# Gathering key and value pages behind the rotary tables' loads, with the page table in a small tile of its own

## The chip, the cores and the metric

The kernel runs on one core of a Trainium2 chip. The metric is the time of one execution on the device in microseconds (us). Engines are named as in the profile: PE is TensorE's matmul stream, PEld its weight loads, DVE is VectorE, ACT is ScalarE, POOL is GpSimd, SP is SyncE. TensorE's clock has two levels, 2.4 GHz (shown as 1.00) and 1.2 GHz (0.50).

## What is computed

One inference step of a two-layer decoder trunk on a prompt of 1024 tokens and 8 sample tokens, f32 in and out. Layer 0 mixes tokens with retention and with a sparse attention whose keys an indexer selects; layer 1 is a gated DeltaNet. Each layer has a modulated mixer and a squared-ReLU MLP. The part that matters here is the indexer of layer 0, and that the sample tokens have a paged cache of 512 past rows (4 pages of 128 rows for each of 8 samples), each row holding key, value and indexer key:

```python
rel = jax.nn.relu(jnp.einsum('bqhd,bkd->bqhk', qi, ki_all).astype(jnp.float32))
score = jnp.einsum('bqhk,bqh->bqk', rel, wi.astype(jnp.float32)) * IDX_DIM ** -0.5
score = jnp.where(causal[None], score, NEG_INF)
_, idx = lax.top_k(score, top_k)
...
k_sel, v_sel = k_all[bidx, idx], v_all[bidx, idx]
logits = jnp.einsum('bqhd,bqkd->bqhk', q, k_sel).astype(jnp.float32) * ATT_DIM ** -0.5
```

## The kernel before

All activations stand transposed, features on partitions and 1032 tokens along the free axis. A dense product is three matmuls per weight block (high part by high part, high by low, low by high, line 188), so that f32 accuracy comes out of a faster matmul type; weights come by SP's DMAs (line 175), and ScalarE and VectorE split them (lines 176, 177).

The token mixer of layer 0 starts in `even_proj`. It projects the index queries and index key (`iqT`, `ikT`), applies the rotary tables (`rope`, its last VectorE step is line 945), reloads two table tiles `cs` from the DRAM input `tabs` (line 1049) and a block of constants (line 155), and transposes the indexer weights into `iwn`. Then a loop (lines 1059 to 1076) makes the prompt's index scores: for each of six row blocks, up to two stretches of 512 keys and four heads there is one matmul with 64 rows (line 1067) into one of two PSUM banks, a Relu that evicts it on ScalarE (line 1070), and a multiply-add on VectorE. These are called score products below.

`gather_pages` (lines 1445 to 1454) copies the sample's pages out of the pool. It loads the page table into SBUF (line 1449), and then, 32 times, GpSimd reads one entry into a register (line 1453) and starts a copy of one page, 160 KB, from DRAM to DRAM into the buffers `pages0` to `pages7` (line 1454). The page table lies in `kn_`, tile W3, which is also scratch for the rope of the second index query. `sample_scores` then takes, for each sample, the index keys of its four pages (`load_pages`, line 1458, in turn into W2 and W3), transposes them (line 1496), multiplies (line 1499), and ends with the scores `SS` (line 1504). In W3 lie also the index keys that line 1082 writes out, so page 1's load comes after that output. `SS` and the prompt's scores feed a search for the threshold (32 rounds, from line 1366 on; line 1385 compares once a round), which runs on VectorE and ScalarE beside the dense products of the attention projections AV and AQ that follow.

The order of each engine's instructions is that of a scheduler at build time, which takes the program's order, priorities and its own estimates. So an instruction that moves in the program moves others. GpSimd issues in its order: DMAs on tables, gathers, page loads and outputs stand in one queue, and one that waits holds those behind it.

```python
self.gather_pages(kn_[0:1, 768:800])
...
v = nc.gpsimd.value_load(ptab[0:1, 4 * b + i:4 * b + i + 1], min_val=0, max_val=a['cache_kv'].shape[1] - 1)
nc.gpsimd.dma_start(self.pages[b][i], a['cache_kv'][0][bass.ds(v, 1)].rearrange("o p r -> (o p) r"))
```

Of the kernel before, what the change touches and what calls it, by code (L numbers as in the profile page):

```python
# [133 lines left out]
class _Step:  # L134
# [852 lines left out]
    def even_proj(self, mis, w, S, SS, aqS, akS, avS, aqD, akD, vD):  # L987

        nc, tc, a = self.nc, self.tc, self.a
# [6 lines left out]
        cs = t(N[8], N[9])  # L996
        rq, rk = _ring(*t(W[4], W[5])), _ring(*t(N[10], W[0]))
        rg_, vn_, kn_ = t(W[1], W[2], W[3])
# [47 lines left out]
        self.blk = BLK  # L1046
        self.consts(1, N[5])
        for i in range(2):
            nc.gpsimd.dma_start(cs[i], a['tabs'][i])
        iwn = mis(128, 9, 4)  # L1050
        p = self.side('tn')
        for c in range(9):
# [6 lines left out]
        for r in range(2, 8):  # L1059
            n = 128 * (r + 1)  # L1060
            for k0 in range(0, n, 512):
                kw = min(512, n - k0)
                dst = S[r][:, k0:k0 + kw]
                for h in range(4):
# [4 lines left out]
                    x = on().rearrange("p c e -> p (c e)")  # L1069
# [6 lines left out]
            nc.vector.tensor_tensor(dst, dst, self.c('cm'), op=OP.min)  # L1076


        self.gather_pages(kn_[0:1, 768:800])
        self.natural(ikT, kn_[:, :512].rearrange("p (c r) -> p c r", c=8), 'tn', rows=64)  # L1080
        kv = a['kv_prompt'][0, 0].rearrange("(c p) r -> p c r", p=128)
        nc.gpsimd.dma_start(kv[:, :, 256:320], kn_[:, :512].rearrange("p (c r) -> p c r", c=8))
# [1148 lines left out]
```

## Time and profile before

| what | value |
| --- | --- |
| median of 3 runs | 2978.12 us (2976.19 to 2978.9) |
| the profiled execution | 2991.83 us |
| its span, first to last instruction | 2990.2 us |
| mean granted clock of TensorE | 0.981 |
| busy: PE / DVE / ACT / POOL | 96% / 66% / 42% / 8% of the span |

The profile is of one execution, 13.7 us above the median of the runs. Times inside it count from its first instruction. A row of the stage table gives, for a stretch, each engine's busy time and the granted clock; a row of the timeline gives one instruction or several equal ones in a line (x4), with the idle time ahead of it in brackets and what ended that; a row of waits says which instruction waited for whom. Line numbers are those of the kernel before.

### The profile page before, as it was taken

What the parts mean: (1) busy time and instruction counts of PE and PEld (TensorE: products, weight loads), DVE (VectorE), ACT (ScalarE), POOL (GpSimd) and SP (SyncE); (2) the same over time, 40 slices, a digit from 0 to 9 for tenths busy, and PEclk for the clock granted to TensorE, in tenths of its full rate; (3) what the DMA queues carried; (4) which work ended last, traced back from release to release, by engine and by line L of the source; (5) the groups of instructions that cost most, each with busy time, mean ns of one, the idle gap of its engine ahead of it and who ended that gap; (6) DMA issues with size and microseconds to landing.
All of it is one profiled execution on the core that took longest, in us unless ns stands there. A gap on an engine that the chain in (4) does not pass through costs nothing. (4 is left out here: it accounts for less than half of the span.)

```text
span 2990.2 us, 57153 instructions
## 1 busy us (share of the span) xinstructions
PE 2878.2 (96%) x22980; PEld 2684.1 (90%) x22980; DVE 1966.3 (66%) x5147; ACT 1245.8 (42%) x2498; POOL 240.8 (8%) x328
## 2 busy tenths in 40 slices
PE   8999999999899999999999999999999999999997
PEld 6559997799799999999988999999998999999997
DVE  4569897448755765454677766764768657765557
ACT  4457734426733431111364565542348434321111
POOL 0210002100000000000001111111100000000002
PEclk9989998999999999999999999998999999999998
DMA  8665325213433556552221222223524426343222
GB/s 277 189 201 142 86 72 177 78 50 106 155 121 128 194 168 191 170 164 94 62 83 40 65 62 49 60 77 113 170 82 129 158 96 205 124 141 106 72 71 65
DMA packets 282678, 358.50 MB, mean 120 GB/s; under 512 B 49494, under 2 KB 230523, under 8 KB 281644
## 3 DMA queue, kind: packets, MB, share of 16 engines
q1 hardware_dynamic: 258786, 272.86, 30.3%
q0 software_dynamic: 23296, 81.85, 8.4%
q8 instruction: 180, 2.95, 0.4%
q14 instruction: 86, 0.70, 0.1%
q10 hardware_dynamic: 330, 0.13, 0.0%
HBM read 271.45 MB, written 80.12 MB: 118 GB/s over the span
## 5 line engine op out<-in xcount | busy, mean ns | idle before, releaser
L188 PE MATMUL bank<-XH,whi 128*128 128x256 f32 (+4 forms) x3488 | 906.3, 305 | 1.9 <-ACT N L1268 0.8
L188 PE MATMUL bank<-XH,wlo 128*128 128x384 f32 (+5 forms) x2720 | 825.5, 304 | 0.9 <-DVE wlo L177 0.9
L188 PE MATMUL bank<-XL,whi 128*128 128x256 f32 (+5 forms) x2976 | 792.6, 302 | 2.2 <-DVE XL L426 1.9
L188 PEld LDWEIGHTS bank<-XH,whi 128*128 128x128 f32 (+1 forms) x3488 | 604.2, 188 | 24.2 <-issue 11.1
L188 PEld LDWEIGHTS bank<-XL,whi 128*128 128x128 f32 (+1 forms) x2976 | 525.7, 188 | 17.8 <-issue 9.5
L188 PEld LDWEIGHTS bank<-XH,wlo 128*128 128x128 f32 (+2 forms) x2720 | 511.7, 188 | 7.8 <-issue 5.0
L638 DVE SCALAR_TENSOR_TENSOR N<-bank,G,N 128x256 f32<-128x256 f32 x576 | 274.8, 481 | 312.6 <-PE bank L188 311.5
L176 ACT CAST whi<-raw 128x1024 fp32r<-128x1024 f32 x142 | 147.5, 1039 | 443.2 <-PE bank L188 397.8
L188 PE MATMUL bank<-W,whi 128*128 128x260 f32 (+1 forms) x1152 | 207.7, 282 | 2.9 <-DVE accS L646 1.5
L177 DVE TENSOR_TENSOR wlo<-raw,whi 128x1024 fp32r<-128x1024 f32 x142 | 173.2, 1220 | 45.6 <-ACT whi L176 44.8
L704 PE MATMUL bank<-W,whi 128*128 128x256 f32 x1094 | 182.9, 284 | 12.4 <-ACT whi L697 7.3
L704 PE MATMUL bank<-W,wlo 128*128 128x256 f32 x1082 | 182.0, 284 | 9.5 <-ACT wlo L697 4.2
L704 PE MATMUL bank<-XH,whi 128*128 128x260 f32 x896 | 181.2, 285 | 8.1 <-ACT N L719 3.0
L704 PE MATMUL bank<-XH,wlo 128*128 128x260 f32 x896 | 181.2, 285 | 4.4 <-DVE wlo L691 3.0
L188 PEld LDWEIGHTS bank<-W,whi 128*128 128x128 f32 x1152 | 176.0, 188 | 8.3 <-DVE N L638 2.5
L697 ACT CAST whi<-raw 128x512 fp32r<-128x512 f32 x168 | 103.9, 622 | 170.9 <-PE bank L704 60.3
L704 PEld LDWEIGHTS bank<-W,whi 128*128 128x128 f32 x1094 | 155.0, 188 | 18.8 <-ACT whi L697 9.5
L704 PEld LDWEIGHTS bank<-W,wlo 128*128 128x128 f32 x1082 | 154.5, 188 | 14.6 <-ACT wlo L697 5.7
L188 PE MATMUL bank<-W,wlo 128*128 128x256 f32 (+1 forms) x576 | 162.0, 283 | 0.5 <-DVE wlo L177 0.5
L691 DVE TENSOR_TENSOR whi<-raw,whi 128x512 fp32r<-128x512 f32 x168 | 115.1, 688 | 67.4 <-ACT whi L697 63.6
L697 ACT CAST wlo<-raw 128x512 fp32r<-128x512 f32 x168 | 103.3, 621 | 133.8 <-PE bank L704 50.4
L691 DVE TENSOR_TENSOR wlo<-raw,wlo 128x512 fp32r<-128x512 f32 x168 | 114.6, 687 | 63.0 <-ACT wlo L697 60.5
(628 smaller groups left out, 5461.0 us busy)
## 6 DMA issues: line engine op xcount, KB each, us to landing
raw<-in_mlp_up_dram SPq DMA_DIRECT2D x96, 512.0 KB, 4.2
N<-in_ada_w_dram SPq DMA_DIRECT2D x80, 512.0 KB, 5.3
W<-hD SPq DMA_DIRECT2D x64, 516.0 KB, 4.4
raw<-in_mlp_down_dram SPq DMA_DIRECT2D x60, 512.0 KB, 3.5
hD<-N POOLq DMA_DIRECT2D x32, 520.0 KB, 4.0
N<-resD SPq DMA_DIRECT2D x32, 512.0 KB, 4.6
hD<-N POOLq DMA_DIRECT2D x32, 512.0 KB, 3.6
raw<-in_odd_w_in_dram SPq DMA_DIRECT2D x32, 512.0 KB, 4.2
```

The lines of the kernel that those rows point to most:

```text
L176: nc.scalar.copy(hi[:, :k * m], raw[:, :k * m])
L177: nc.vector.tensor_tensor(lo[:, :k * m], raw[:, :k * m], hi[:, :k * m], op=OP.subtract)
L188: self.nc.tensor.matmul(out, ww[:, i, ms], xx[:, c0:c1], start=start and i == 0 and j == 0, stop=stop and i == nk - 1 and j == 2)
L638: nc.vector.scalar_tensor_tensor(r, ps[:, :256], g[:, dt, 0:1], r, op0=OP.mult, op1=OP.add)
L691: sub = lambda o, x, y: V.tensor_tensor(o, x, y, op=OP.subtract)
L697: nc.scalar.copy(hi, a)
L704: nc.tensor.matmul(o, ww[:, k], xx, start=start and k == 0 and n == 0, stop=k == 3 and n == 2, skip_group_check=True)
```

## The change

`gather_pages` is called right behind the two loads of the rotary tables, and no longer after the score loop. `issue_after(x.ins)` lets the scheduler issue its instructions only behind the second table's load. The page table goes into a piece of 32 words of the tile of small things (`mis`, M), where it was part of W3. Nothing else is edited; lines of the changed kernel are 2 higher from line 1050 to the end of the score loop, and 1 higher from there on.

```diff
         for i in range(2):
-            nc.gpsimd.dma_start(cs[i], a['tabs'][i])
+            x = nc.gpsimd.dma_start(cs[i], a['tabs'][i])
+        with tc.issue_after(x.ins):
+            self.gather_pages(mis(1, 32))
         iwn = mis(128, 9, 4)
...
-        self.gather_pages(kn_[0:1, 768:800])
         self.natural(ikT, kn_[:, :512].rearrange("p (c r) -> p c r", c=8), 'tn', rows=64)
```

On GpSimd, from the tables' loads on, the order before is this (TENSOR_LOAD reads a page table entry, `N_97` is the block of constants, `W_90` is W3):

```order
L1049 DMA N_99<-in_tabs_dram 128x1032
L155 DMA N_97<-in_cst_dram 128x951
L1482 DMA iwD<-M 8x4
L1483 DMA W_96<-iwD 32x1
L1449 DMA W_90<-in_page_table_dram 1x16x2
L1453 TENSOR_LOAD W_90
L1453 ISA x2
L1454 ISA
L1454 DMA pages_994<-in_cache_kv_dram 16x2560
```

And after the change:

```order
L1049 DMA N_99<-in_tabs_dram 128x1032
L1450 DMA M<-in_page_table_dram 1x16x2
L1454 TENSOR_LOAD M
L1454 ISA x2
L1455 ISA
L1455 DMA pages_857<-in_cache_kv_dram 16x2560
L1454 TENSOR_LOAD M
L1454 ISA x2
L1455 ISA
L1455 DMA pages_857<-in_cache_kv_dram 16x2560
L155 DMA N_97<-in_cst_dram 128x951
```

The page table and two of the 32 gathers now stand ahead of the constants' load, 30 behind it; the index weights' detour through DRAM (iwD) has gone behind the gathers. At the end of the gathers the order is, after the change:

```order
L1455 DMA pages_864<-in_cache_kv_dram 16x2560
L1083 DMA out_dram<-W_90 128x8x64
L1483 DMA iwD<-M 8x4
L1459 DMA W_89<-pages_857 128x4x64
L1459 DMA W_90<-pages_858 128x4x64
L1484 DMA W_96<-iwD 32x1
L1459 DMA W_89<-pages_859 128x4x64
```

Before, the page loads followed the output of W3 in the same way, without the two iwD rows between them.

On PE the orders are the same up to row 531. There the order before goes on as follows (rows 529 to 536), with products of AV (128x264):

```order
L188 MATMUL bank_69<-XH,wlo_83 128x384
L1067 MATMUL bank_73<-N_100,W_92 128x512
L1067 MATMUL bank_74<-N_100,W_92 128x512
L188 MATMUL bank_70<-XH,whi_80 128x264
L188 MATMUL bank_70<-XL,whi_80 128x264
L188 MATMUL bank_70<-XH,wlo_83 128x264
L188 MATMUL bank_70<-XH,whi_80 128x264
L188 MATMUL bank_70<-XL,whi_80 128x264
```

After the change the pages' transposes stand there (rows 529 to 539):

```order
L188 MATMUL bank_69<-XH,wlo_83 128x384
L1069 MATMUL bank_73<-N_100,W_92 128x512
L1069 MATMUL bank_74<-N_100,W_92 128x512
L1497 MATMUL bank_71<-cst,W_89 64x128 x4
L1497 MATMUL bank_72<-cst,W_90 64x128
L1069 MATMUL bank_73<-N_100,W_91 128x128
L1497 MATMUL bank_72<-cst,W_90 64x128 x2
L1069 MATMUL bank_74<-N_100,W_91 128x128
L1497 MATMUL bank_72<-cst,W_90 64x128
L188 MATMUL bank_70<-XH,whi_80 128x264
L1500 MATMUL bank_76<-W_89 32x512
```

The first page's transposes have moved from row 583 to row 532, with 28 score products still to come. Between rows 532 and 594 stand all eight pages' transposes and products and 8 matmuls of line 188; before, rows 532 to 637 held 54 of line 188 among them, 24 of 128x264 and 30 of 128x384. The rest of AV follows in one piece from row 596 (128x264), and the search's rounds begin earlier among VectorE's and ScalarE's instructions. From the attention on, the orders agree.

## Rows read from the trace of the kernel before

**Rows 1.** Page of the profile, part 1: busy us and share by engine.

```profile
PE 2878.2 (96%) x22980; PEld 2684.1 (90%) x22980; DVE 1966.3 (66%) x5147; ACT 1245.8 (42%) x2498; POOL 240.8 (8%) x328
```

**Rows 2.** Stages: length, busy us (instructions) by engine, clock, DMA share, GB/s.

```profile
117.20:139.70 22.50, 22.19 (x77) 10.54 (x76) 15.73 (x31) 14.82 (x32) 9.58 (x19) 1.00 0.52 156
139.70:146.50 6.80, 0.00 (x0) 0.00 (x0) 2.28 (x3) 0.98 (x2) 2.93 (x4) 0.62 0.69 183
146.50:165.20 18.70, 18.66 (x45) 7.50 (x46) 6.51 (x13) 3.88 (x7) 3.68 (x6) 0.50 0.26 84
...
400.00:475.00 75.00, 71.24 (x489) 69.50 (x488) 73.48 (x202) 16.83 (x34) 5.87 (x9) 1.00 0.31 87
```

**Rows 3.** Timeline of GpSimd (POOL), 60 to 152 us: start, length, line; idle before.

```profile
72.34 0.53 POOL L1049 DMA_DIRECT2D N<-in_tabs_dram  x1 [8.82 <-PE bank L416]
81.40 0.54 POOL L155 DMA_DIRECT2D N<-in_cst_dram  x1 [8.54 <-DMA resD<-N]
...
95.86 0.51 POOL L1449 DMA_DIRECT2D W<-in_page_table_dram  x1 [3.85 <-DVE W L945]
103.00 0.50 POOL L1454 DMA_DIRECT2D pages<-in_cache_kv_dram  x1 [6.63 <-DVE N L1072]
...
111.53 0.49 POOL L1454 DMA_DIRECT2D pages<-in_cache_kv_dram  x1 [1.06 <-issue]
...
139.78 0.49 POOL L1454 DMA_DIRECT2D pages<-in_cache_kv_dram  x1 [0.67 <-issue]
140.47 0.94 POOL L1082 DMA_DIRECT2D out_dram<-W  x1 [0.21 <-issue]
141.40 0.91 POOL L1458 DMA_DIRECT2D W<-pages  x1
145.89 0.75 POOL L1458 DMA_DIRECT2D W<-pages  x1 [3.58 <-DMA out_dram<-W]
```

**Rows 4.** What PE waited for, 60 to 190 us: total, times, longest.

```profile
PE bank L1496 <- DMA W<-pages: 6.9, 1, 6.9
```

**Rows 5.** Timeline of PE, 105 to 180 us: start, length, line; idle before.

```profile
117.19 0.39 PE L188 MATMUL bank<-XH,whi 128*128 128x264 f32 x1
117.42 0.28 PE L188 MATMUL bank<-XL,whi 128*128 128x264 f32 x1
...
146.54 0.85 PE L1496 MATMUL bank<-cst,W 128*64 128x128 f32 x3 [6.89 <-DMA W<-pages]
...
152.11 1.91 PE L1499 MATMUL bank<-W 64*32 64x512 f32 x2
...
172.05 1.04 PE L1499 MATMUL bank<-W 64*32 64x512 f32 x2
173.11 0.63 PE L1496 MATMUL bank<-cst,W 128*64 128x128 f32 x4
```

**Rows 6.** What weight loads waited for, 117.2 to 139.7 us.

```profile
PEld bank L1067 <- ACT N L1070: 6.8, 14, 0.8
```

**Rows 7.** GpSimd DMAs, 103 to 140 us: KB each, median us to landing.

```profile
pages<-in_cache_kv_dram POOLq DMA_DIRECT2D x32, 160.0 KB, 2.5
```

**Rows 8.** GpSimd DMAs, 146 to 156 us, same columns.

```profile
W<-pages POOLq DMA_DIRECT2D x3, 128.0 KB, 2.6
```

**Rows 9.** PE by stretches: length, busy us, granted clock, DMA share, GB/s.

```profile
38.80:42.30 3.50, 3.50 (x16) 0.51 1.05 317
```

**Rows 10.** VectorE (DVE) by stretches, same columns.

```profile
80.00:100.00 20.00, 13.16 (x18) 1.00 0.68 185
103.00:140.00 37.00, 25.56 (x47) 1.00 0.64 190
```

**Rows 11.** What PE waited for, 177.5 to 475 us.

```profile
PE bank L1234 <- ACT N L1226: 5.0, 4, 2.4
PE bank L1285 <- DVE N L1280: 1.7, 1, 1.7
```

**Rows 12.** Timeline of DVE, 174 to 186 us.

```profile
179.06 0.17 DVE L1385 TENSOR_TENSOR M<-M 128x7 f32<-128x7 f32 x1
```

## The prediction

> **What bounds the kernel now.** The profiled execution took 2991.83 us (span 2990.2). TensorE is busy 2878.2 us, 96% [rows 1], so time is won or lost only where it waits, where its matmuls run longer than they need, or where its clock is low. I went from the stage table to the waits, then to the two timelines that meet at the stop.
>
> The stage table [rows 2] shows one hole: from 139.7 to 146.5 us PE executes nothing. The table of PE's waits gives it one cause, 6.9 us for the first page tile [rows 4]. The GpSimd timeline says why it is late [rows 3]: the 32 gathers run from 103.00 to 139.78, one every 36.78 / 31 = 1.186 us, though each lands in about 2.5 us [rows 7]; the issuing is the limit. The loop begins only after the page table, issued at 95.86 behind DVE's rope (L945, whose output shares the buffer), and PE has score products enough to run until 139.7. The chain ends 141.40 (page 0's load) to 146.54 (transpose): 5.14 us.
>
> Behind the hole lies a second loss. The granted clock is 0.50 (1.2 GHz) from 146.5 to 165.2, 18.70 us, of which PE is busy 18.66 [rows 2]. A page's key product takes 1.91 us there and 1.04 us at full clock [rows 5]. So 18.70 us at half clock did 9.35 us of work. The whole late gather costs 6.9 + 9.35 = 16.25 us.
>
> The third loss is small: from 117.2 to 139.7 the score products alternate over two PSUM banks and each waits for its Relu eviction on ScalarE, 14 waits and 6.8 us in the weight loads' table [rows 6]. PE is shown busy 22.19 of 22.5 us there [rows 2], so a product that waits there must count as a long one.
>
> **The change, part by part.** *The gather moves up on GpSimd.* No instruction is added but one tile M; the page table no longer waits for L945. The last rotary table is issued at 72.34 to 72.87 [rows 3], so the page table's DMA issues there. From page table issue to first gather took 103.00 - 95.86 = 7.14 us; hence first gather at 80.0, at 82.5 if its landing is late. After two gathers the constants' DMA (L155) waits for what it waited for before, and was ready at 81.40, so costs only its issue of 0.54. Thirty gathers at 1.186 us end at about 117.8. Then the index-key output (0.94, it was already waiting in line before), the iwD issue (about 0.5), and page 0's load is issued at about 119.5. With the 5.14 us seen, PE could resume at 124.7; with the late ends 127.5.
>
> *The page work moves up on PE too*, because the scheduler re-planned with an earlier gather: the first transposes stand at row 532 instead of 583. PE passes row 531 at 117.19 [rows 5]. So the gather comes 22 us earlier and its consumer 22 us earlier as well: the wait is 124.7 - 117.2 = 7.5. Page 1's buffer is the one the index keys are written out from, so its load waited 145.89 - 140.47 = 5.42 us from that output's issue [rows 3]; now that ends at 118.0 + 5.4 = 123.4, and with the 2.6 us of a page load [rows 8] page 1 is there at 126.0, when the 0.63 us of page 0's transposes [rows 5] are over for 0.7, of which I count 0.5 as a wait. In all 8.0 against 6.9, **+1.1**. If the page table lands late, +3.9; if output and pages land sooner, at best about -1, since one load's 2.6 us after 119.5 is the least.
>
> *The score stretch is filled.* After the wait the 28 remaining score products share PE's order with 8 page rounds, each a key product of 1.04 and transposes of 0.63, that is 8 x 1.67 = 13.4 us of work [rows 5] between products that waited 6.8 us for evictions. The AV products that filled them before come in one block afterwards, where nothing holds them. Bounds: 0 (the page rounds wait for the same ScalarE, which copies each transposed page) to -6.8. I take **-5.5**, nearer the row, since page work is twice the waits.
>
> *The clock.* A stop as long as before is followed by half clock again; the only other short stretches at half clock near here last 3.5 us [rows 9]. I take the same 18.7 us, **0**; bounds -7.6 (3.5 us) and the slower rival.
> The Trainium skill (TensorE: Matmul & The Clock Gate, What's actually happening) says the throttled state is the default and that activity releases it; the 18.66 us of busy at 0.50 [rows 2] show that being busy alone did not release it here, so by that rule the sum would be near -14, with the -7.6 bound, and by the row it is -6.4; I keep the row.
>
> *The search starts earlier.* The threshold search of 32 rounds fills DVE up to the attention: 73.48 of 75 us in 400 to 475 [rows 2]. Its first comparison is at 179.06 [rows 12]; it needs the sample scores, which end some 13 us earlier after the change. Later PE waits that DVE and ACT cause in 177.5 to 475 are 5.0 and 1.7 us [rows 11]. From the attention on the orders are the same. I take **-2**, bounds -6.7 (all go) and +3 (the AV and AQ evictions meet a busier ScalarE and DVE).
>
> Sum: 1.1 - 5.5 + 0 - 2 = -6.4. On the profiled 2991.83 that gives 2985.4; the median of the runs is 13.7 lower, and as the loss lies in one stage I carry the difference over whole: 2978.12 - 6.4 = 2971.7, say **2972 us**. 0.2% is 6.0 us, about what a measurement of this kernel can tell from no change.
>
> **Rivals.** *Nothing comes of it* (about 2978): the wait moved with its consumer and the page rounds are bound by the evictions they were to hide, or half clock lasts 30 us, (30 - 18.7) / 2 = 5.6 us, which takes back the 5.5. For it: 6.8 us of waits are on the same ScalarE that copies the pages. Against: ScalarE was busy 14.82 of 22.5 us there [rows 2].
>
> *Slower, the clock stays low.* Before, after the hole, 128-row products of L188 were mixed in and the clock rose at 165.2. Now 28 score products on 64 rows and page work on 64 columns follow the hole with only 8 products of L188 up to row 594. If only dense products raise the clock, it stays at half until they return: the score products (22.19 busy less 24 x 0.28 of L188 = 15.5 us) and 13.4 of page work are 28.9 us at full, some 55 at half. That costs (55 - 18.7) / 2 = 18 more than before, less the 6.4, and some 2 that the evictions hide: +10, **2988**. It decides from 43 us at half clock on ((43 - 18.7) / 2 = 12.2, less 6.4, is 0.2%). For it: the same mixture with few L188 left ran at 0.50 from 146.5 on. Against: score products alone kept 1.00 until 139.7 [rows 2].
>
> *The wait vanishes*: page 0 is there when PE comes, and clock loss with it, -16.25, **2962**. This asks the gather to be done 7.5 us sooner than the issue rate allows; DMA was at most 0.68 busy [rows 10], so not by transfer. That the change does not do what it says, because L155 holds 30 gathers behind it, gives a later end by the time its release slips; released at 81.40 as before, that is nothing.
>
> *GpSimd slowed by DVE.* The gathers now run beside 80 to 100 us, where DVE is busy 13.16 of 20. Before they ran beside 25.56 of 37 [rows 10], 69% against 66%, and only one gap had grown, by 0.4 us [rows 3]. I count 0 and, were every gather of those 20 us to grow so, 17 x 0.4 = 6.8 us of delay, in the range.
> The Trainium skill (SBUF — State Buffer, Who interferes with whom) says that a DVE instruction in a 2-port mode and GpSimd lock each other out of a shared port pair; the even spacing beside a busy DVE shows no such cost, and by the rule every gather that met a lock would end late and the wait would be longer by up to some 7 us.
>
> **How the numbers follow.** Forecast 0.45, its own range -11 to -3; of this 0.33 is past 6.0 us, 0.12 within. Nothing comes of it, a slowed GpSimd counted with it (-6.4 + 6.8 = +0.4), 0.26, within. Slower 0.22. Vanishing wait 0.07, faster. So faster 0.40, same 0.38, slower 0.22. The range of 2963 to 2988 leaves out the vanishing wait and the half of the slower case beyond +10, together 0.18.
>
> **What would show it.** Right: a wait of 7 to 10 us for the first page at 117 in PE's table, gathers from 80 to 118, the stretch of half clock after about 125 lasting 15 to 25 us, ScalarE's waits in the score products much less than 6.8, the search's first comparison at about 165. Wrong: no wait at 117 (vanishing); half clock past 168 (slower); gathers spaced well over 1.2 us (DVE); a first gather after 82.5.

## The result and the profile after

The changed kernel is slower: 3006.3 us median of 6 runs (2988.26 to 3011.92) against 2977.15 us of the kernel before in the same sessions (6 runs, 2970.32 to 2979.43). The ratio is 1.0095, with a 95% interval of 1.0075 to 1.0115. The profiled execution took 3011.92 us (span 3010.2). Single runs of this kernel spread over some 20 us, and the mean granted clock goes with them (0.983 in the fastest, 0.973 to 0.978 in the others), so the traces below are read for mechanisms and the medians for sizes.

First where the time is lost. The rows are the first and the last of 32 transposes at the start of retention, a fixed place in the program: the kernel before, then the changed one. Each row ends with the start of the first and the last of the group.

```profile
L1234 PE MATMUL bank<-cst,N x32: 270/274/332, 299.3 to 483.2; 128*128 128x128 f32 x32
```

```profile
L1235 PE MATMUL bank<-cst,N x32: 271/328/477, 315.6 to 504.3; 128*128 128x128 f32 x32
```

The changed kernel is 16.3 us behind at the first and 21.1 at the last; the whole span differs by 20.0. So most of the loss lies ahead of 300 us, and a little more comes up to 480 us, where this trace has two more stretches at half clock, of some 7 us each from 318 and from 441 us, and that of before has none. The medians differ by more than the traces, 29.2 us, since the profiled execution of before was 14.7 us above its median here and that of the changed kernel 5.6 us above its own. The stage table of 100 to 190 us, of the kernel before and then of the changed one (columns as in [rows 2]), says what kind of loss it is.

```profile
100.00:190.00 90.00, 79.99 (x307) 39.90 (x305) 46.45 (x97) 41.32 (x84) 26.98 (x47) 0.87 0.55 163
```

```profile
100.00:190.00 90.00, 80.05 (x222) 35.24 (x221) 42.59 (x83) 33.84 (x69) 17.96 (x30) 0.66 0.36 113
```

PE is busy for as long as before, 80.05 against 79.99 us, but at a mean granted clock of 0.66 in place of 0.87: (0.87 - 0.66) x 90 = 18.9 us of full-speed work less. PE does not wait longer; it runs slower. PE's stage table of the changed kernel (columns as in [rows 9]) shows when:

```profile
109.90:120.10 10.20, 10.20 (x21) 0.50 0.84 263
120.10:127.00 6.90, 4.41 (x17) 0.99 0.61 189
127.00:164.50 37.50, 34.71 (x72) 0.50 0.06 16
164.50:174.80 10.30, 8.26 (x30) 1.00 0.27 84
174.80:188.40 13.60, 13.60 (x44) 0.50 0.34 115
```

Three stretches at half clock, 10.2 + 37.5 + 13.6 = 61.3 us, where the trace of the kernel before had one of 23.9 us (141.3 to 165.2 by its clock record; PE stood still in the first 5 us of it). What counts is PE's busy time in them: 10.20 + 34.71 + 13.60 = 58.5 us against the 18.66 of [rows 2]. Half of the excess, (58.5 - 18.7) / 2 = 19.9 us, is work lost to the clock. It is the same clock record as in the means just read, and agrees with their 18.9.

The GpSimd timeline of the changed kernel has the gather where it was meant to be:

```profile
73.09 0.52 POOL L1450 DMA_DIRECT2D M<-in_page_table_dram  x1
81.22 0.52 POOL L1455 DMA_DIRECT2D pages<-in_cache_kv_dram  x1 [7.61 <-issue]
...
120.38 0.49 POOL L1455 DMA_DIRECT2D pages<-in_cache_kv_dram  x1 [0.66 <-issue]
...
122.65 0.79 POOL L1459 DMA_DIRECT2D W<-pages  x1
125.67 0.76 POOL L1459 DMA_DIRECT2D W<-pages  x1 [2.23 <-DMA iwD<-M]
```

It is 22 us earlier than in [rows 3], at one gather per 39.16 / 31 = 1.263 us. But its transfers now run beside the index key's rope, whose halves are swapped by SP's DMAs. From issue to landing the index key's two swaps took 2.4 us before, and 3.6 us after the change:

```profile
W<-W SPq DMA_DIRECT2D x2, 129.0 KB, 2.4
```

```profile
W<-W SPq DMA_DIRECT2D x2, 129.0 KB, 3.6
```

VectorE's timeline shows the last add of that rope before, at 97.25, and after the change, at 100.49, behind a wait for the swap:

```profile
97.25 1.23 DVE L945 TENSOR_TENSOR N<-N,W 64x1032 f32<-64x1032 f32 x1
```

```profile
99.22 1.23 DVE L944 TENSOR_TENSOR W<-W,W 64x1032 f32<-64x1032 f32 x1 [1.86 <-DMA W<-W]
100.49 1.23 DVE L945 TENSOR_TENSOR N<-N,W 64x1032 f32<-64x1032 f32 x1
```

PE's timeline of the changed kernel then has two groups of stops and a single one, and behind the second group score products at half speed:

```profile
101.77 0.91 PE L1069 MATMUL bank<-N,W 64*128 64x384 f32 x2 [0.89 <-DVE N L945]
...
108.23 0.91 PE L1069 MATMUL bank<-N,W 64*128 64x384 f32 x2 [1.30 <-DMA N<-N]
...
122.59 1.61 PE L1069 MATMUL bank<-N,W 64*128 64x512 f32 x4 [0.31 <-ACT N L1072]
125.95 0.62 PE L1497 MATMUL bank<-cst,W 128*64 128x128 f32 x4 [1.75 <-DMA W<-pages]
128.38 0.39 PE L1497 MATMUL bank<-cst,W 128*64 128x128 f32 x1 [1.80 <-issue]
...
135.70 2.08 PE L1069 MATMUL bank<-N,W 64*128 64x512 f32 x4
...
156.69 5.21 PE L1069 MATMUL bank<-N,W 64*128 64x384 f32 x8 [0.20 <-ACT N L1072]
...
174.28 0.66 PE L1497 MATMUL bank<-cst,W 128*64 128x128 f32 x4 [1.16 <-DMA W<-pages]
```

The first stops, at 101 and 108 us, are waits for the late index key (L945 and the DMA that doubles it), and the clock falls at 109.9. The second, at 124 and 127 us, are waits for the first two page tiles, and the clock, back since 120.1, falls again at 127.0. The page stop is short: 1.75 + 1.80 = 3.55 us, where the kernel before waited 6.89 [rows 5]. What stands behind it runs at half speed until 164.5, where the clock comes back among score products. A wait of 1.16 us for a later page, at 173 us, stands ahead of the third stretch.

The question for the experiments: is it the gather's traffic, the new order of PE, the stop, or two of them together?

### The profile page after: what moved, and what is told of

It is laid out like the page before. It is cut to its first block, busy times and chain, and to the rows that moved or that the text cites. A ratio compares the mean times of both kernels' runs of the same rounds, so it can differ in the third digit from the quotient of the medians.

```text
span 3010.2 us, 57138 instructions
## 1 busy us (share of the span) xinstructions
PE 2895.3 (96%) x22980; PEld 2694.1 (89%) x22980; DVE 1967.6 (65%) x5147; ACT 1245.0 (41%) x2498; POOL 240.1 (8%) x328
## 5 line engine op out<-in xcount | busy, mean ns | idle before, releaser
L697 ACT CAST whi<-raw 128x512 fp32r<-128x512 f32 x168 | 103.9, 622 | 164.6 <-PE bank L704 59.2
```

What stands on the lines that cost most here:

```text
L697: nc.scalar.copy(hi, a)
```

## The experiments

Three theories were set against each other: **contention** (the gather's transfers delay the rope, and that is the loss), **order** (few dense products, which are those of 128 rows of line 188, between score products and page work keep the clock low by themselves), and, after the first four runs, **a stop ahead of sparse work** (the order does no harm while the clock is high; after a stop it does not bring it back).

### The own tile alone

The kernel before, with this edit:

```diff
-        self.gather_pages(kn_[0:1, 768:800])
+        self.gather_pages(mis(1, 32))
```

> The kernel before with only the page table in its own small tile; the call stays behind the score loop. The scheduler then puts the page table and all 32 gathers on GpSimd ahead of the rotary tables' loads, right behind the first constants (in the kernel before GpSimd is idle from 2 to 63 us), and the page work early in PE's order (first page transposes at row 499). So nothing of the gather runs beside the index key's rope, and no page is waited for, but PE's order is as sparse as in the changed kernel. Theory 'order' (28 score products and the page work with few dense products between them keep the granted clock at 0.50): a long stretch at 0.50 again, 2985 to 3005 us. Theory 'contention' (the gather's transfers delay the rope's swaps, PE stops at 100 to 108 us, the clock falls there and that is the loss): rope's last add at about 97, clock 1.00 through 120, 2960 to 2970 us. Rival: the gather takes DMA time from the first weights (DMA share 0.91 to 0.99 from 10 to 40 us), 3 to 10 us lost before 60 us.

Measured: 2977.55 us (10 runs), ratio 0.9993 [0.9971, 1.0016]. The order of PE is as sparse as the changed kernel's, and yet the time is that of the kernel before: the theory "order" alone falls. "Contention" expected 2960 to 2970, and this is not that either. The rival named last shows in the GpSimd timeline: the second rotary table, issued at 72.34 in [rows 3], comes 7.9 us later here. With the gather at the start PE waits 6.9 us for the first weights (line 342), where it waited 1.0 us before.

```profile
80.26 0.53 POOL L1049 DMA_DIRECT2D N<-in_tabs_dram  x1 [8.85 <-PE bank L416]
```

So it seems that the stage gave back some 8 us and that the start took them. Its stretches around the sparse work (stage table, columns as in [rows 2]) are at half clock for only about 10 us, in 116 to 126, behind a wait of 1.1 us for a page, and from the middle of the sparse work on at full clock, through work that is as sparse:

```profile
117.00:130.00 13.00, 13.00 (x28) 4.40 (x27) 7.22 (x11) 7.22 (x14) 2.23 (x3) 0.65 0.29 78
130.00:140.00 10.00, 9.91 (x37) 4.14 (x37) 7.81 (x16) 6.38 (x16) 0.98 (x2) 1.00 0.26 68
140.00:150.00 10.00, 9.21 (x30) 3.07 (x29) 6.42 (x13) 6.61 (x15) 1.26 (x2) 1.00 0.09 26
```

### The changed kernel with the page work held back on PE

```diff
+                    if (r, k0, h) == HOLD:
+                        self.held = y.ins
...
-            for i in range(4):
-                nc.tensor.transpose(p[:64, 128 * i:128 * i + 128], pg[:, i], self.ident)
+            with self.tc.issue_after(self.held):
+                for i in range(4):
+                    nc.tensor.transpose(p[:64, 128 * i:128 * i + 128], pg[:, i], self.ident)
```

(`y` is the score product's instruction, and `HOLD` is `(7, 512, 1)`.)

> The changed kernel with the pages' transposes queued on PE behind the score product of block 7, keys 512 to 1023, head 1, which gives nearly PE's order of the kernel before (same up to the first page transposes). The gather still runs from 81 to 120 us. Theory 'order': page waits go, the dense products between score products are back, the stop at 100 to 108 us costs some 3 us and half clock of about 10 us; no stretch of 0.50 of over 15 us, 2965 to 2978 us. Theory 'contention': the clock that fell at 110 us stays at 0.50 until the score products end, 25 us and more, 2980 to 2990 us. If GpSimd's page ring is the loss: as the changed kernel, over 2995 us.

Measured: 2976.22 us (10 runs), ratio 0.9977 [0.9955, 0.9999]. With the gather as early as in the changed kernel, but PE's old order, 25 to 30 us of the changed kernel's time (3001.32 and 3006.3 in its two series) are gone, as the theory "order" had it. The rope is late here too (its last add comes at 99.76) and the clock falls once, at 103.9 us, for 17.1 us; from 121 to 185 us it is at 1.00. So the early gather costs a stretch at half clock, but not the long one. "Contention" as the whole loss falls. The edit took away the stop for the first pages together with the sparse order, so it does not tell these two apart.

### Other traffic beside the swaps of the kernel before

```diff
+        with tc.issue_after(self.cdma.ins):
+            dm = self.dr.tile([16, 128, 320], F32, name='dummy')
+            for i in range(12):
+                nc.gpsimd.dma_start(dm[i], a['cache_kv'][0][i])
```

(`self.cdma` is the constants' load.)

> The kernel before with 12 copies of 160 KB (static pages to a DRAM scratch buffer nobody reads) issued by GpSimd behind the constants' load, about 82 to 89 us, so beside the index key's swaps; all orders are otherwise those of the kernel before, and the gather itself starts when it did. Theory 'contention': the index key's last add (97.25 us before, 100.49 after) comes 1 to 3 us late, PE stops as in the changed kernel before 110 us, the clock falls there and the time is 2990 us or more. Theory 'order': the same late add and stop, but the clock is back within some 10 us since the dense products stand between the score products, then the known stop for the page: 2978 to 2986 us. If the swaps do not suffer: 2977 us.

Measured: 2975.05 us (10 runs), ratio 0.9976 [0.995, 1.0002]. The add of the rope came at 98.40, 1.15 us later than in the kernel before and so less late than in the changed kernel (3.24 us). No stretch at half clock lies at 100 to 110 us, and nothing was lost. The run is weaker evidence than it was meant to be, since the copies hit the swaps less than the gather does. It showed something else. The stop for the first page was as long as ever (7.16 us), but the half clock lasted only 6.8 us, where the trace of the kernel before has 23.9:

```profile
143.40:150.20 6.80, 3.53 (x10) 0.50 0.41 130
```

What follows a stop at half clock is thus not one number, even with the same order: PE's instructions are those of the kernel before, in its order throughout. What ran behind the stop until the clock came back was page transposes and score products, without one dense product:

```profile
146.67 0.85 PE L1500 MATMUL bank<-cst,W 128*64 128x128 f32 x3 [7.16 <-DMA W<-pages]
147.45 2.08 PE L1071 MATMUL bank<-N,W 64*128 64x512 f32 x4
149.46 0.83 PE L1500 MATMUL bank<-cst,W 128*64 128x128 f32 x3
150.22 1.12 PE L1071 MATMUL bank<-N,W 64*128 64x512 f32 x2
```

### The own tile, gather at the start, page work held

The kernel of the second experiment without `issue_after` around the gather, which lets the scheduler put it at the start as in the first.

> Own tile with the gather where the scheduler puts it without any constraint (ahead of the rotary tables' loads, right behind the first constants), and PE's page work held as in e2_held. Both theories: no contention at 81 to 100 us, no page wait, dense products between score products; the 6.9 us stop and the 9.35 us of half clock of the kernel before go: 2960 to 2966 us. Against e1_own_tile_alone only PE's order differs, so theory 'order' expects 20 to 40 us between the two, theory 'contention' under 5. If the gather hurts the first weights, both lose 3 to 10 us before 60 us.

Measured: 2977.24 us (10 runs), ratio 0.9992 [0.9966, 1.0018]. The forecast of 2960 to 2966 us missed for the reason it named: the second rotary table is issued at 81.20, 8.9 us later than before. Against the first experiment, held or not held made no difference that could be measured (2977.24 and 2977.55): where PE hardly waits for pages, the sparse order costs nothing to speak of. That led to the third theory.

### The changed kernel with a faster gather

```diff
+                if i:
+                    nc.gpsimd.dma_start(self.pages[b][i], a['cache_kv'][0][4 * b + i])
+                    continue
```

> The changed kernel, every engine's order kept as it is but GpSimd's: three of each sample's four pages are copied from fixed places instead of those that the table names, so 24 of 32 table reads are left out and the gather is issued in some 24 us instead of 39. Pages are then in SBUF by about 113 us, before PE comes for them at 124; the transfers still run beside the index key's rope, denser than before. Theory 'stop ahead of sparse work' (PE's stop for pages at 123 to 128 us drops the clock, and the score products and page work behind it do not raise it again): no stop, no stretch at 0.50 from 127 to 164, about 2970 to 2980 us. Theory 'order with contention' (the sparse order itself, entered after the rope's delay, keeps the clock low): a stretch at 0.50 of 30 us or more again, 2995 us or more.

(PE's place of the page work is pinned where the changed kernel has it, by the rule of the second experiment on an earlier score product. The kernel leaves out 24 reads of the page table, so it scores other pages than the table names, and only its time is of use.)

Measured: 2986.2 us (10 runs), ratio 1.0021 [0.9998, 1.0045]; the changed kernel has 1.0095. That lies between the two forecasts. PE's timeline at the places of the changed kernel's:

```profile
108.39 1.65 PE L1072 MATMUL bank<-N,W 64*128 64x384 f32 x2 [1.58 <-DMA N<-N]
...
124.31 1.61 PE L1072 MATMUL bank<-N,W 64*128 64x512 f32 x4 [0.31 <-ACT N L1077]
125.86 0.74 PE L1506 MATMUL bank<-cst,W 128*64 128x128 f32 x5
...
130.41 1.13 PE L1072 MATMUL bank<-N,W 64*128 64x512 f32 x4
...
143.69 3.32 PE L1072 MATMUL bank<-N,W 64*128 64x384 f32 x8 [0.20 <-ACT N L1077]
```

The first stop is there, and so is the first stretch at half clock. At 125.86 the pages are there and PE does not stop. The same four score products take 1.13 us in place of 2.08, the same eight 3.32 in place of 5.21. PE's stage table:

```profile
108.30:122.00 13.70, 13.61 (x27) 0.50 0.68 188
122.00:159.50 37.50, 33.93 (x121) 1.00 0.15 42
159.50:173.20 13.70, 13.70 (x44) 0.50 0.34 116
```

In this trace 37.5 us of sparse work run at 1.00 with PE busy 33.93 us; in the changed kernel's, 37.5 us of it run at 0.50 with PE busy 34.71. PE's instructions are the same in both, in the same order from start to end. What differs on PE is the short stop for pages: both traces of the changed kernel (the second is below) have it and the long stretch behind it, and this one has neither. The time stays a little above the kernel before, as the first and the last of the three stretches at half clock remain.

### A stop without the gather beside the rope

The first experiment's kernel, and on GpSimd around page 0's load 16 copies (of 128 bytes each, not of 8 as the expectation says):

```diff
+            if b == 0:
+                dd = self.dr.tile([16, 32], F32, name='late')
+                for q in range(16):
+                    nc.gpsimd.dma_start(dd[q:q + 1], z[0:1, 0:1].rearrange("p b r -> p (b r)"))
```

> e1_own_tile_alone with 16 copies of 8 bytes, read by nobody, on GpSimd's queue around page 0's load, so that page 1 comes some 7 us late: a stop of PE without any gather beside the rope. What follows the stop is nearly the changed kernel's sparse order. Theory 'stop ahead of sparse work': a stretch at 0.50 of over 25 us behind the stop, some 7 + 13 us more than e1_own_tile_alone (2977.6), 2992 to 3002 us. Theory 'contention': the stop's 7 us and at most 5 for the clock, 2980 to 2989 us.

Measured: 3008.33 us (6 runs), ratio 1.0094 [1.0065, 1.0122]. That is 31 us more than the kernel without the 16 copies, from another session, and more than either theory gave. PE's order is that of the first experiment only up to 120 us; behind that the scheduler made another, as sparse. The stop that it makes is 3.55 us, and the stretch at half clock behind it is the longest of all:

```profile
128.69 0.82 PE L1500 MATMUL bank<-cst,W 128*64 128x128 f32 x3 [3.55 <-issue]
```

```profile
108.00:126.30 18.30, 17.14 (x61) 1.00 0.80 156
126.30:191.20 64.90, 60.20 (x134) 0.50 0.14 41
```

No gather runs beside the rope here, so contention is not needed for the loss.

### Gather behind the index weights, page work held

The page table is in its own tile, and the gather is called in `sample_scores` behind the second copy of the index weights, so after the swaps; PE's page work is held as in the second experiment.

```diff
-        nc.gpsimd.dma_start(iw, iwD.rearrange("b (h o) -> (b h) o", o=1))
+        y = nc.gpsimd.dma_start(iw, iwD.rearrange("b (h o) -> (b h) o", o=1))
+        with self.tc.issue_after(y.ins):
+            self.gather_pages(self.ptab)
```

> Page table in its own tile, loaded as early as GpSimd can; the gather queued on GpSimd behind the two copies of the index weights, so from about 92 to 130 us, after the index key's swaps; PE's page work held as in e2_held. Both theories: no gather beside the swaps, no stop for pages (loads at about 132 to 138, PE comes at about 139), so the 6.9 us stop and its half clock go: 2962 to 2970 us. If the times of the kernels so far (2975 to 2978) mean that something later takes the gain back, 2975 again.

Measured: 2970.17 us (10 runs), ratio 0.9974 [0.9955, 0.9993], the upper end of what was expected. Once more, in a later session:

> e7_behind_iw_held once more with more rounds, beside the changed kernel on one chip: 2968 to 2973 us, ratio to the kernel before 0.995 to 0.998; its profile again without a stop for pages and without a stretch at 0.50 between 100 and 200 us.

Measured: 2968.26 us (12 runs), ratio 0.9964 [0.9944, 0.9984] to 2979.17: 10.9 us faster than the kernel before, and the best of all kernels. PE's only wait for a page in this run is one of 0.8 us. Its stage table has no half clock in the whole region, and the fixed place in the program comes at 282.3 us:

```profile
100.00:140.00 40.00, 39.57 (x140) 1.00 0.67 198
140.00:200.00 60.00, 54.64 (x312) 1.00 0.73 228
```

```profile
L1239 PE MATMUL bank<-cst,N x32: 270/274/477, 282.3 to 465.5; 128*128 128x128 f32 x32
```

That is 17.0 us ahead of the profiled execution before. The prediction had priced the stop and its half clock at 16.25 us. The medians differ by less, 10.9 us, which fits a profile whose half clock was on the long side (23.9 us, against 6.8 in the third experiment's trace of the same order).

The second and the fourth experiment and these two runs have one and the same order on PE throughout and differ in the place of the gather: beside the swaps 2976.22 us, at the start 2977.24, behind the swaps 2970.17 and 2968.26. So the gather's traffic has a price of its own, 6 to 8 us by these medians, though the intervals of the ratios overlap. Beside the swaps the rope's last add comes at 99.76 and 17.1 us of half clock follow; behind them it comes at 96.23 and none does.

### The same gather, page work free

> e7_behind_iw_held without the rule that queues the pages' transposes behind a late score product: page table in its own tile, gather behind the index weights' copies, the scheduler free. The first page transposes then stand 11 instructions after where they stood held, with few dense products between the score products that are left. Pages land at about 138 us, when PE comes. Theory 'stop ahead of sparse work': most score products are done by then, so only a short sparse piece can follow a stop: within 5 us of e7_behind_iw_held, 2968 to 2976 us. If holding the page work was what paid: 2976 us or more.

The edit is the one above without the rule on PE's page work. Measured: 2990.81 us (10 runs), ratio 1.0028 [1.0007, 1.0049], a miss of the expectation: holding the page work is worth 22.5 us against the run of the same session. Left to its own estimates, the scheduler puts the first transposes so early that PE waits 6.1 us for them. The waits of PE and its stage table:

```profile
PE bank L1498 <- DMA W<-pages: 6.1, 1, 6.1
```

```profile
117.00:135.00 18.00, 13.84 (x50) 1.00 0.53 149
135.00:172.50 37.50, 34.09 (x75) 0.50 0.24 68
```

My error was to take the sparse piece behind the stop for short. It is the third trace with a stop ahead of sparse work and a long half clock. Dense products stood in the later part of it: 11 of the 75 matmuls at 0.50.

### The changed kernel again

> The changed kernel unedited, for a second trace: theory 'stop ahead of sparse work' expects a stop for pages at 122 to 129 us again, behind it a stretch at 0.50 of over 25 us, and 3000 to 3012 us. If this trace has the stop but no such stretch, the theory falls.

Measured: 3001.32 us (7 runs), ratio 1.0068 [1.0043, 1.0093]. Its trace has the page stop (2.3 + 0.7 us) and behind it half clock from 130.3 for 34.1 us and from 167.9 for 23.9 us; the first fall, after the late index key, is at 103.0 for 17.1 us.

### Dense work added

```diff
+            fb = self.side('a')
+            with self.tc.issue_after(x.ins):
+                for i in range(8):
+                    nc.tensor.transpose(fb[:, 0:128], self.ident, self.ident)
```

(`x` is the last transpose of the page.)

> The changed kernel with 8 transposes of the 128x128 identity (dense, into a free PSUM bank, read by nobody) on PE behind each page's transposes, 64 in all, about 7 us of added work at full clock; the scheduler moves a few dense products too. Theory 'sparse work keeps the clock low': the added dense work raises the clock within the stretch, at most 20 us at 0.50 behind the stop in place of 37.5 and 13.7, so not slower than the changed kernel in spite of the added work: 2990 to 3005 us. If the clock does not depend on it: 7 to 14 us slower than the changed kernel, 3013 to 3020 us.

Measured: 3000.16 us (8 runs, 2984.99 to 3016.44), ratio 1.0082 [1.0053, 1.0111]. The median lies where the theory "sparse work keeps the clock low" put it, but the runs lie on both sides, and the profiled one is the fastest of them: in it the clock is at 1.00 from 118.9 to 187 us. But in that execution PE waits for no page, so there was no stop ahead of the page work. It is one more trace of full clock without a stop, and says nothing of dense work behind one; the slower executions have no trace. Whether dense work raises the clock here was not settled.

## Why the prediction was wrong

It said 2972 us, 2963 to 2988, and 0.40 for faster. The rival on the other side, "slower, the clock stays low", is what happened, with a chance of 0.22 and a price of 2988 that was too low.

**The step that failed** is the term of the clock: "A stop as long as before is followed by half clock again ... I take the same 18.7 us, 0". PE was busy at half clock for 58.5 us, in three stretches, where the term has 18.7, and that cost (58.5 - 18.7) / 2 = 19.9 us of work against the trace of before. The stop was not as long as before but half as long, 3.55 us, and the stretch behind it was longer, 37.5 us: the length is not a property of the stop. Behind about the same page stop in the order of before it was 23.9 us and 6.8 us (third experiment); behind stops of 3.0 to 6.1 us ahead of sparse work it was 37.5, 34.1, 64.9 and 37.5 us. The other two stretches, 10.2 and 13.6 us, stand behind stops that the prediction did not have, for the late index key and for a later page. The rival came near with its half clock of some 55 us, but then took 8 us of gains off that did not come. Its condition, that only dense products raise the clock, the runs do not bear out: in the third experiment's trace, and at 164.5 us in the changed kernel's, the clock came back among score products and page work.

**The evictions**, -5.5: the gain did not come, and the waits doubled. The table of what weight loads waited for, 117 to 190 us, has 14.9 us in 17 waits for the Relu evictions; before it has 7.2 in 15 there, nearly all of it in [rows 6]. The low clock is not the reason, as the same order at full clock (the faster gather, 117 to 165 us) has 13.2 us in 21 waits:

```profile
PEld bank L1069 <- ACT N L1072: 14.9, 17, 2.3
```

The page work stands in few lumps between the products, and not one piece behind each, and the dense products that had filled the waits are gone.

**The search's start**, -2: it was to begin at about 165 and began later than in [rows 12], as the sample scores ended later:

```profile
185.62 0.17 DVE L1386 TENSOR_TENSOR M<-M 128x7 f32<-128x7 f32 x1
```

**The wait**, +1.1: wrong in sign and of no weight. The first gather came at 81.22, within the 80.0 to 82.5 said; the gathers took 1.263 us in place of 1.186, which is 2.4 us in all, some 0.7 of it the constants' issue among them, and far from the 6.8 that the rival "slowed by DVE" allowed; page 0's load was issued at 122.65, not 119.5. PE, though, was 7 us late itself, at 124.2 in place of 117.2, and waited only 3.55 us. That lateness is a mechanism that the prediction did not have: it looked for the gather's contention with GpSimd's issue and found none, took the DMA share of 0.68 at 80 to 100 us [rows 10] for room (it is 0.81 after the change), and did not ask whose transfers share the DMA engines there. They are the index key's swaps. A gather took 4.7 us to land there (median of 31) where [rows 7] have 2.5:

```profile
pages<-in_cache_kv_dram POOLq DMA_DIRECT2D x31, 160.0 KB, 4.7
```

The Trainium skill (DMA: Bandwidth & Descriptors, Queues, rings and completion order) says that each DMA engine takes turns between the queues that have work for it. By that rule the gather's packets take turns with those of the swaps. The trace agrees in that both took longer to land, the swaps 3.6 us in place of 2.4 and a gather 4.7 in place of 2.5; no row here shows the turns themselves.

What was right: that the consumer moved up as far as the gather, so that the wait would not vanish; that the clock had to be a term of the sum, with a rival for its failing; and, at least for the profiled executions, the price of the late gather, 16.25 us: the version with the gather behind the swaps is 17.0 us ahead in its trace. By the medians it is 10.9.

The Trainium skill (TensorE: Matmul & The Clock Gate, What's actually happening) says that the throttled state is the default and that activity releases it. The traces show PE busy at both levels: 34.71 of 37.5 us at 0.50 in the changed kernel, 33.93 of 37.5 at 1.00 with the faster gather, in the same order of instructions. The rule agrees with these two traces in that a stop came ahead of each of their falls from 100 to 190 us. That both levels can last through the same work, no run here explains.

Shown is that the changed kernel loses its time to the clock, and that the stop for pages is needed for the long stretch: with PE's order kept and the stop gone, the stretch went and the time fell from 3006.3 and 3001.32 to 2986.2. All four series with a stop of 3.0 to 6.1 us ahead of sparse work are slow (3006.3, 3008.33, 2990.81, 3001.32), and the sparse order with a stop of 1.1 us is not (2977.55). That the sparse order is needed as well is argued only from the kernel before, which has the longer stop in a denser order: no pair of runs changed the order and kept the stop.

What stays open: why the clock stays low so long behind these stops, why the stretch behind one stop varies (6.8 to 23.9 us), and why the changed kernel's runs spread from 2988 to 3012 us. Nor is a stop the only way to a fall. Later in the trace of the best kernel's second series the clock falls with PE busy all the time, ahead of the fall and in it:

```profile
512.00:524.00 12.00, 12.00 (x91) 9.96 (x90) 5.02 (x16) 6.36 (x12) 3.10 (x5) 1.00 0.66 219
524.40:541.40 17.00, 17.00 (x63) 13.79 (x64) 5.33 (x19) 3.90 (x9) 1.54 (x3) 0.50 0.19 58
```

## What to carry to other kernels

When a producer is moved up under a scheduler, compare the orders for where the consumer went; if it moved as far, the wait has only moved, and pinning the consumer may be worth more than the earlier start (22.5 us here). Before a stop is moved, ask what PE runs behind it, and do not carry the old loss over: the stretches of 34 to 65 us at half clock all stood behind a stop ahead of 64-row products and transposes to 64 columns, though that this work is the reason is not shown. Ask also whose transfers the moved DMAs will run beside; of the places tried here the gather was best not at the earliest but behind the swaps, and just early enough.

## What the runs showed of the hardware that was not expected

With the same order of instructions on PE, 37.5 us ran at a granted clock of 0.50 behind a stop of 3.55 us, and 37.5 us at 1.00 without the stop. The clock also fell, for 17 us, behind 12 us in which PE was busy throughout. A gather of 5 MB between two places in DRAM delayed small transfers inside SBUF: the index key's two swaps took 3.6 us to land in place of 2.4, and the last add of the rope behind them came 3.24 us later. And a gather on an idle queue at the very start of the kernel was not free: the second rotary table was issued 7.9 and 8.9 us later in the two kernels that had it there, with 6.9 and 5.7 us of waits for the first weights in place of 1.0.
